# A hybrid decoder block on one core: where four of its modulation sums, the prefix sum of log f and some small transposes are computed

## The chip, the cores and the metric

The kernel runs on one core of a Trainium2 chip, as one launch. The metric is device time in microseconds; the time given for a kernel is the median of its runs. One more execution is recorded by the hardware profiler. Its span reaches from the first to the last instruction, and its own time is a little longer.

## What is computed

A decoder block for one sequence, all in float32, cut to what matters here. `mod` is the adaptive modulation: silu(c) times a 1024 x 6144 matrix, six vectors of 1024.

```python
mod = silu(c) @ w_ada + b_ada
sh1, sc1, g1, sh2, sc2, g2 = split(mod, 6)

h = rmsnorm(x, norm1_g) * (1 + sc1) + sh1
cb, cc, cv, q, k, v, f_logit, ga, gb = split(h @ w_in, IN_OFFSETS)
ya = cb * causal_dwconv(cc * cv, conv_a_w)
q, k = rmsnorm(q per head, q_norm_g), rmsnorm(k per head, k_norm_g)
log_f = log_sigmoid(f_logit + b_f)
F = cumsum(log_f, axis=sequence)           # 1024 positions x 8 heads
yb = softmax(q k^T / 8 + F[t] - F[s], causal) v
merged = sigmoid(ga) * (ya @ w_branch_a) + sigmoid(gb) * (yb @ w_branch_b)
x = x + g1 * (merged @ w_out)

h2 = rmsnorm(x, norm2_g) * (1 + sc2) + sh2
gate, val = split(causal_dwconv(h2 @ w_up, conv_ffn_w), 2)
x = x + g2 * ((silu(gate) * val) @ w_down)  # d_ff = 2816
```

## The kernel before

Sequence and model width are 1024, so x, h and most weights come as eight blocks (ND, NT) of 128. A product of float32 matrices is made of three matmuls on a high and a low part of each operand (TERMS: high x high, high x low, low x high). ACT copies the high part out (wsplit L93, h_tile L309), DVE or POOL subtract it to get the low part (L94, L312 on POOL, L315 on DVE).

Stages, in the span's time. **Head** (0 to 42 us): x is loaded, normed, transposed. **k loop** (to about 80): for dd = 1 to 7 one block of the contraction of k for seven tokens of 128 positions (k_mm, L326). Each step needs the modulation's shift and scale for block dd. These come from `ada_mul` (L220): two 512 KB blocks of w_ada, in [128 x 2 x 128] slices for eight k, are scaled by silu(c) and summed by DVE into two accumulators in SBUF, the even and the odd slices (two tensor_scalars L224, six scalar_tensor_tensors L226), and these are added (L229). `ada_sum` (L235) then sums over the partitions by two matmuls of one column against ones, into the bank `pm`. h_mod on ACT takes a and b from it, h_tile makes h's next block. With every odd dd, POOL splits the next unit of w_in (L94). In steps 3 to 5 a row of conv weights (`rw`) is transposed on PE, in step 6 the two norm gains (`rg`).

**V phase** (91 to 148): v for eight tokens, eight steps each (`tok_mm`, L530). **Q phase** (148 to 213): q for eight tokens. In both, small work is placed by hand: `at(t, f)` calls f before the matmuls of step t; steps count from TV = 8 for v and from TQ = 72 for q, eight to a token, about 0.7 us each in Q. So a token's sum of squares, root and norm (`sums`, `root`, `norm` on DVE), its transposition (`turn`, PE, qT), and its high and low parts (`high` on ACT, `low` on DVE, L493) stand at offsets from its first step. The remaining modulation blocks, the list `rest` (columns 16 to 47 in pairs), are loaded by `rest_load`, multiplied in four parts by DVE, ACT and POOL (`rest_mul`: L434, L437 on DVE, L438 ACT, L439 and L441 POOL), and summed over partitions by `late_pm`: five pairs in V, six in Q (NQ), five in the stage behind. `log_f`, `f_sum` and `f_turn` make the prefix sum F: f_sum multiplies log f by an upper triangle (`pf`) and by ones (`po`), and adds the totals of the blocks of 128 positions by eight small DVE operations; f_turn transposes it.

Behind that come the other products of w_in (to 350 us), attention (to 640), the mixing, the **up projection** (to about 1241; per f of 22 a tile of 128 gate and 128 value columns, by seven half-size products p1 to p7) and the **down projection** (77 steps of about 2.72 us). In a tile of the up projection the sums of DVE named c11, u2, u34, c12 and c21 put the products together, `scale`, `taps` and `silu` apply the convolution to the tile before, and `ff` multiplies its halves. POOL sums weights (L1593 to L1604), ACT and DVE split them (L1559, L1560).

Inside `manual_schedule` the order of the code is the order on each engine; SP, which issues most transfers, is ordered by hand in the head, k, V and Q phases, and by the scheduler in the up projection. The lines that steer the pieces named above:

```python
rest, rest_open, rest_sum, rest_acc = list(range(16, 48, 2)), [], [], []
at(t0 + 12, late_pm)      # V
at(TQ + 19, f_sum)
at(TQ + 21, f_turn)
at(t0 + 16, late_pm)      # Q
```

## Time and profile before

| what | value |
|---|---|
| time, median of 3 runs | 1474.64 us (1472.72 to 1478.87) |
| the profiled execution | 1473.5 us, span 1471.5 us |
| PE busy | 1403.4 us, 95% |
| DVE / ACT / POOL busy | 1099.4 / 651.8 / 504.1 us |
| mean granted clock of TensorE | 0.989 |
| DMA | 222.44 MB, mean 151 GB/s |

The page's first part gives an engine's busy time; what it does not tell is when the engine was idle, and that is read from the windows and timelines. In a timeline a row is one instruction or a run of equal ones, with start, duration, engine, line and names, and in square brackets the idle time ahead of it and what ended that. PE's fp32 matmul is run as two instructions, so a `pm` pair is shown as x4. The granted clock (PEclk) is a share of full speed.

### The profile page before, as it was taken

To read this page: it belongs to the slowest core of one execution; us is meant where nothing else is said; L and a number is where in the kernel's file an instruction comes from. 1 tells how busy PE (TensorE), PEld (TensorE's weight loads), DVE (VectorE), ACT (ScalarE), POOL (GpSimd) and SP (SyncE) were. 2 spreads that over 40 slices of the span, in tenths; PEclk is the share of its full clock that TensorE was granted. 3 is DMA by queue.
4 is the path that set the end of the run, shared out by engine and by line. 5 is a ranking of instruction groups with operands and counts; after the bars stand their busy time and mean duration, and the time that the engine had idled before them with its cause. 6 is when DMAs were issued, how large, how long until landed. Compare 5 with 4: busy or idle time off the path is not lost. (4 is left out here: it accounts for less than half of the span.)

```text
span 1471.5 us, 19375 instructions
## 1 busy us (share of the span) xinstructions
PE 1403.4 (95%) x6668; PEld 1155.1 (78%) x6668; DVE 1099.4 (75%) x1828; ACT 651.8 (44%) x1104; POOL 504.1 (34%) x532
## 2 busy tenths in 40 slices
PE   5889889999999999899999999999999999999997
PEld 4679668887888888778788877888888887888876
DVE  7965798888777776456846858777777776898764
ACT  6554453434455454555414534333333333444443
POOL 3646666665555553323221013333333331000000
PEclk9999999999999999999999999999999999999999
DMA  9539654437664557776962122222222213983722
GB/s 286 160 105 322 199 163 129 132 95 209 159 169 115 146 133 227 225 244 219 244 164 83 44 72 86 86 87 86 86 86 86 72 36 116 390 311 103 213 80 77
DMA packets 260759, 222.44 MB, mean 151 GB/s; under 512 B 43117, under 2 KB 213445, under 8 KB 260661
## 3 DMA queue, kind: packets, MB, share of 16 engines
q1 hardware_dynamic: 259389, 218.61, 49.6%
q0 software_dynamic: 1136, 2.56, 0.6%
q8 instruction: 52, 0.85, 0.2%
q14 instruction: 46, 0.38, 0.1%
q10 hardware_dynamic: 136, 0.04, 0.0%
HBM read 169.76 MB, written 51.41 MB: 150 GB/s over the span
## 5 line engine op out<-in xcount | busy, mean ns | idle before, releaser
L1925 PE MATMUL dn<-bL,aH 128*128 128x512 f32 x308 | 120.5, 391 | 0.6 <-DVE bL L1919 0.6
L1925 PE MATMUL dn<-bH,aH 128*128 128x512 f32 x308 | 120.8, 392 | 0.0
L1925 PE MATMUL dn<-bH,aL 128*128 128x512 f32 x308 | 120.0, 390 | 0.0
L1559 ACT ACTIVATE wh<-ws 128x512 fp32r<-128x512 f32 x95 | 55.5, 627 | 133.8 <-POOL ws L1593 131.0
L730 DVE TENSOR_TENSOR ol<-ws,oh 128x512 fp32r<-128x512 f32 x98 | 94.6, 974 | 14.1 <-ACT oh L729 11.6
L94 DVE TENSOR_TENSOR wl<-ws,wh 128x1024 fp32r<-128x1024 f32 (+1 forms) x51 | 70.0, 1373 | 40.6 <-ACT wh L93 40.1
L729 ACT ACTIVATE oh<-ws 128x512 fp32r<-128x512 f32 x98 | 61.2, 626 | 70.9 <-PE pacc L775 38.6
L1593 POOL TENSOR_TENSOR ws<-ws 128x512 f32<-128x512 f32 x19 | 24.7, 1300 | 187.7 <-DVE wl L94 187.7
L1162 ACT ACTIVATE L<-L,mn 128x256 f32<-128x256 f32 (+6 forms) x56 | 46.4, 829 | 60.7 <-DVE mn L1160 58.9
L1165 POOL TENSOR_SCALAR L<-L,rs 128x384 f32<-128x384 f32 (+7 forms) x62 | 48.3, 779 | 69.8 <-DVE rs L1164 68.6
L1925 PEld LDWEIGHTS dn<-bL,aH 128*128 128x128 f32 x308 | 57.8, 188 | 14.1 <-DVE bL L1919 2.7
L1185 ACT ACTIVATE th<-pt 128x512 fp32r<-128x512 f32 (+1 forms) x80 | 43.5, 551 | 55.3 <-PE pt L1179 53.7
L559 POOL TENSOR_TENSOR ws<-ws 128x512 f32<-128x512 f32 x42 | 55.1, 1312 | 36.5 <-DVE ol L730 17.1
L1925 PEld LDWEIGHTS dn<-bH,aH 128*128 128x128 f32 x308 | 57.8, 188 | 12.3 <-ACT bH L1918 0.4
L1925 PEld LDWEIGHTS dn<-bH,aL 128*128 128x128 f32 x308 | 57.8, 188 | 11.9
L93 ACT ACTIVATE wh<-ws 128x1024 fp32r<-128x1024 f32 (+1 forms) x58 | 60.8, 1052 | 12.3 <-DMA ws<-in_w_branch_a_dram 4.1
L1560 DVE TENSOR_TENSOR wl<-ws,wh 128x512 fp32r<-128x512 f32 x76 | 64.2, 864 | 2.3 <-ACT wh L1559 2.3
L1918 ACT ACTIVATE aH<-dws 128x512 fp32r<-128x512 f32 x52 | 32.8, 631 | 74.6 <-issue 41.0
L1680 DVE SCALAR_TENSOR_TENSOR u<-upv,cwT,u 128x1023 f32<-128x1023 f32 (+1 forms) x44 | 56.4, 1282 | 10.7 <-ACT u L1676 9.9
L1186 DVE TENSOR_TENSOR tl<-pt,th 128x512 fp32r<-128x512 f32 (+1 forms) x80 | 50.3, 634 | 18.5 <-ACT th L1185 17.1
L439 POOL TENSOR_TENSOR wacc<-wacc,wa 128x256 f32<-128x256 f32 x48 | 43.5, 907 | 55.8 <-ACT wa L438 52.4
L1919 DVE TENSOR_TENSOR aL<-dws,aH 128x512 fp32r<-128x512 f32 x52 | 35.9, 690 | 34.2 <-ACT aH L1918 34.2
(561 smaller groups left out, 4503.0 us busy)
## 6 DMA issues: line engine op xcount, KB each, us to landing
wa<-in_w_ada_dram SPq DMA_DIRECT2D x48, 512.0 KB
dws<-in_w_down_dram SPq DMA_DIRECT2D x96, 256.0 KB
ws<-in_w_up_dram SPq DMA_DIRECT2D x44, 512.0 KB
ws<-in_w_in_dram SPq DMA_DIRECT2D x36, 512.0 KB
ff<-ff_d SPq DMA_DIRECT2D x44, 256.0 KB
ff_d<-u SPq DMA_DIRECT2D x21, 512.0 KB
xt<-in_x_dram SPq DMA_DIRECT2D x8, 512.0 KB
v_d<-vt SPq DMA_DIRECT2D x8, 512.0 KB
```

Source lines behind the costliest of these rows:

```text
L93: scalar.activation(wh[:, : n * m], ws[:, : n * m], AF.Copy)
L94: eng.tensor_tensor(out=wl[:, : n * m], in0=ws[:, : n * m], in1=f32(wh[:, : n * m]), op=ALU.subtract)
L559: gpsimd.tensor_tensor(out=o, in0=a, in1=b, op=ALU.subtract)
L729: scalar.activation(h, src, AF.Copy)
L730: eng.tensor_tensor(out=l, in0=src, in1=f32(h), op=ALU.subtract)
L1162: scalar.activation(L[:, :n], L[:, :n], AF.Exp, scale=-1.0, bias=mn, accum_out=sm)
L1165: eng.tensor_scalar(out=L[:, :n], in0=L[:, :n], scalar1=rs, scalar2=0.0, op0=ALU.mult, op1=ALU.add)
L1186: vector.tensor_tensor(out=flat[2][:, c0:], in0=flat[0][:, c0:], in1=f32(flat[1][:, c0:]), op=ALU.subtract)
L1559: scalar.activation(ops[0][:, sl], src, AF.Copy)
L1560: eng.tensor_tensor(out=ops[1][:, sl], in0=src, in1=f32(ops[0][:, sl]), op=ALU.subtract)
L1680: vector.scalar_tensor_tensor(out=u[:, s:], in0=acc[:, : S - s], scalar=cwT[:, 2 - s, n : n + 1], in1=u[:, s:], op0=ALU.mult, op1=ALU.add)
L1925: mm(banks[e], self.A[i][:, es_], self.B[j], start=self.p in FIRST and self.c == 0 and t == 0, stop=self.c == NC - 1 and t == 2, skip_grou ...
```

## The change

- **k's sums.** `hT`, one bank of PSUM, holds pm in its first two columns and an accumulator of 256 columns behind them. `ada_chain` sums all eight slices into this one accumulator, each operation reading what the one before wrote; the eighth writes to SBUF. It is made in two parts around h_tile(dd + 1, 0), and behind h_mod(dd + 1), which reads the same bank.
- **Small transposes.** The rows of the gains and conv weights are loaded into the pool of the V phase, behind the fetches of v's first units. The gains are turned together at step 5, the three rows of conv weights at step 29 with one copy.
- **log f.** f_sum accumulates eight matmuls into pf: the triangle, then ones against ever shorter parts of log f. One DVE copy is left. f_turn comes 13 steps later.
- **Modulation pairs and q tokens.** `rest` ends at column 39, Q takes two pairs instead of six. late_pm comes 3 steps later in V and 6 in Q. The q tokens 0 to 5 go in pairs: one sum, root and norm for two, and two turns in two banks.
- **g2.** Its eight blocks of w_ada (512 KB each) are loaded in the up projection, one per tile from f = 5 on. In the next tile ACT scales the eight slices (four ahead of silu, four behind split4), POOL folds them by three adds to 128 columns, and at step 7 of the down projection (T0 + 1) eight matmuls of one column and one DVE add finish g2.

What stands on DVE in the k loop before (L224, L226, L229: ada_mul; L315: the low part of h):

```order
L224 TENSOR_SCALAR wacc<-wa,cT 128x256 x2
L226 SCALAR_TENSOR_TENSOR wacc<-wa,cT,wacc 128x256 x6
L229 TENSOR_TENSOR wacc<-wacc 128x256
L315 TENSOR_TENSOR h01L_118<-raw_187,h01H_114 128x512
L224 TENSOR_SCALAR wacc<-wa,cT 128x256 x2
```

And now (L238 and L243: the chain; hT is the bank):

```order
L238 TENSOR_SCALAR hT<-wa,cT 128x256
L243 SCALAR_TENSOR_TENSOR hT<-wa,cT,hT 128x256 x6
L243 SCALAR_TENSOR_TENSOR wacc<-wa,cT,hT 128x256
L329 TENSOR_TENSOR h01L_118<-raw_187,h01H_114 128x512
L238 TENSOR_SCALAR hT<-wa,cT 128x256
```

The two forms take the same places; seven of the eight operations now write to PSUM. On PE in the Q phase before, around the first token's transposition (L235 pm, L483 qT, L632 and L634 f_sum):

```order
L530 MATMUL qacc<-wl,h11H_131 128x512
L530 MATMUL qacc<-wh,h11L_135 128x512
L235 MATMUL pm<-ones,wacc 128x1 x2
L483 MATMUL qT<-ident,qn 128x128 x4
L530 MATMUL qacc<-wh,h01H_112 128x512
...
L530 MATMUL qacc<-wh,h01L_118 128x512
L632 MATMUL pf<-lf,upper 128x64
L634 MATMUL po<-lf,ones 128x64
L530 MATMUL qacc<-wh,h01H_115 128x512
```

And now (L658, L660: f_sum; L249 pm; L509 qT; two q tokens per pair):

```order
L556 MATMUL qacc<-wh,h01L_118 128x512
L658 MATMUL pf<-lf,upper 128x64
L660 MATMUL pf<-lf,ones 128x56
...
L660 MATMUL pf<-lf,ones 128x8
L556 MATMUL qacc<-wh,h01H_115 128x512
...
L556 MATMUL qacc<-wh,h11L_133 128x512
L249 MATMUL pm<-ones,wacc 128x1 x2
L556 MATMUL qacc<-wh,h11H_130 128x512
...
L509 MATMUL qT<-ident,qn 128x128 x4
...
L509 MATMUL qT<-ident,qn 128x128 x4
```

pm and the first qT moved behind f_sum, by 26 and 35 rows of PE, and the second token's qT now stands seven rows behind the first. On POOL in a tile of the up projection there were five instructions (L1560 a low part, L1593 to L1604 the sums of weights):

```order
L1560 TENSOR_TENSOR wl<-ws,wh 128x512
L1593 TENSOR_TENSOR ws<-ws 128x512
L1594 TENSOR_TENSOR ws<-ws 128x512
L1599 TENSOR_TENSOR ws<-ws 128x512
L1604 TENSOR_TENSOR ws<-ws 128x512
```

And now eight (L1858: the adds of g2):

```order
L1595 TENSOR_TENSOR wl<-ws,wh 128x512
L1858 TENSOR_TENSOR wa<-wa 128x512
L1858 TENSOR_TENSOR wa<-wa 128x256
L1858 TENSOR_TENSOR g2s<-wa 128x128
L1628 TENSOR_TENSOR ws<-ws 128x512
L1629 TENSOR_TENSOR ws<-ws 128x512
L1634 TENSOR_TENSOR ws<-ws 128x512
L1639 TENSOR_TENSOR ws<-ws 128x512
```

The adds stand between the low part of one weight and the sums for the next tile. The diff:

```diff
@@ -186,9 +186,9 @@
-    def rows_in(srcs, nm, eng=gpsimd, m=P):
-
-        st = xp.tile([P, P], F32, name=nm)
+    def rows_in(srcs, nm, eng=gpsimd, m=P, pool=None):
+
+        st = (pool or xp).tile([P, P], F32, name=nm)
         o = 0
@@ -228,6 +228,20 @@
         return acc[0]
+
+    def ada_chain(wa, part):
+
+        sums = hT[:, 256:512].rearrange("p (i m) -> p i m", i=2)
+        for k in range(4 * part, 4 * part + 4):
+            src, c1 = wa[:, :, k, :], cT[:, k : k + 1]
+            if k == 0:
+                vector.tensor_scalar(out=sums, in0=src, scalar1=c1, scalar2=None, op0=ALU.mult)
+                continue
+            out = sums
+            if k == ND - 1:
+                out = ap.tile([P, 2, P], F32, tag="wacc0", name="wacc", bufs=1)
+            vector.scalar_tensor_tensor(out=out, in0=src, scalar=c1, in1=sums, op0=ALU.mult, op1=ALU.add)
+        return out
@@ -366,25 +380,19 @@
     h_ada(4)
+    hT = aux_tile("hT")
     k_mm(0, (4, 5, 6), TERMS[:1])
-    h_mod(1, ada_sum(wc[1], aux_tile("pm")))
+    h_mod(1, ada_sum(wc[1], hT))
+    ada_chain(was[2], 0)
     k_mm(0, (4, 5, 6), TERMS[1:])
-    qk_rows = []
-    for nm, dst, src, f in (("rk", kg, k_norm_g, 1.0), ("rq", qg, q_norm_g, -0.125)):
-        qk_rows.append((rows_in([src, src], nm, sync, HD), dst, f))
-    cw_rows = [rows_in([conv_ffn_w[0, t].rearrange("(n p) -> n p", p=P)], f"rw{t}", sync) for t in range(3)]
-    wc[2] = ada_mul(was[2])
+    h_tile(1, 0)
+    wc[2] = ada_chain(was[2], 1)
     h_ada(5)
-    h_tile(1, 0)
     h_tile(1, 1)
...
     for dd in range(1, ND):
-        if dd + 2 < ND:
-            wc[dd + 2] = ada_mul(was[dd + 2])
-        if dd + 5 < ND:
-            h_ada(dd + 5)
         if dd == 2:
@@ -397,23 +405,41 @@
             units[dd // 2 + 1] = wsplit(kraw[dd // 2 + 1], gpsimd)
-        h_mod(dd + 1, ada_sum(wc[dd + 1], aux_tile("pm")))
+        h_mod(dd + 1, ada_sum(wc[dd + 1], hT))
+        if dd + 2 < ND:
+            ada_chain(was[dd + 2], 0)
         h_tile(dd + 1, 0)
+        if dd + 2 < ND:
+            wc[dd + 2] = ada_chain(was[dd + 2], 1)
+        if dd + 5 < ND:
+            h_ada(dd + 5)
         h_tile(dd + 1, 1)
         k_mm(dd, range(7), TERMS[1:])
-        if 3 <= dd < 6:
-            scalar.activation(cwT[:, dd - 3, :], rows_T(cw_rows[dd - 3], "rw"), AF.Copy)
-        elif dd == 6:
-            for (st, _), dst, f in qk_rows:
-                pt = aux_tile("rg")
-                tensor.transpose(pt[:HD, 0:2], st[0:2, :HD], ident[0:2, 0:2])
-                for r in range(2):
-                    scalar.activation(dst[r * HD : r * HD + HD], pt[:HD, r : r + 1], AF.Copy, scale=f)
     headS.close()
...
     bp = bS.enter_context(tc.tile_pool(name="qkv", bufs=1, side="right", reuse_waits="tile"))
+
+    qk_rows = []
+    for nm, dst, src, f in (("rk", kg, k_norm_g, 1.0), ("rq", qg, q_norm_g, -0.125)):
+        qk_rows.append((rows_in([src, src], nm, sync, HD, bp), dst, f))
+    cw_rows = [rows_in([conv_ffn_w[0, t].rearrange("(n p) -> n p", p=P)], f"rw{t}", sync, pool=bp) for t in range(3)]
+
+    def gains():
+
+        pt = aux_tile("rg")
+        for i, ((st, _), dst, f) in enumerate(qk_rows):
+            tensor.transpose(pt[:HD, 2 * i : 2 * i + 2], st[0:2, :HD], ident[0:2, 0:2])
+        for i, ((st, _), dst, f) in enumerate(qk_rows):
+            for r in range(2):
+                scalar.activation(dst[r * HD : r * HD + HD], pt[:HD, 2 * i + r : 2 * i + r + 1], AF.Copy, scale=f)
+
+    def cw_turn():
+        pt = aux_tile("rw", "aux2")
+        for t, (st, n) in enumerate(cw_rows):
+            tensor.transpose(pt[:, P * t : P * t + n], st[:n, :], ident[:n, :n])
+        scalar.activation(cwT, pt[:, : 3 * P].rearrange("p (t n) -> p t n", t=3)[:, :, : 2 * NF], AF.Copy)
@@ -448,7 +474,7 @@
-    rest, rest_open, rest_sum, rest_acc = list(range(16, 48, 2)), [], [], []
+    rest, rest_open, rest_sum, rest_acc = list(range(16, 40, 2)), [], [], []
     late_pm = lambda: rest_end(aux_tile("pm", "aux2"))
@@ -586,7 +612,7 @@
     nz, u, w, lw, m, num, den, lf = (small(n) for n in "nz u w lw m num den lf".split())
-    tot, Fs = nz, w
+    Fs = w
     FT = bp.tile([64, P], F32, name="FT")
@@ -629,15 +655,10 @@
         pf = aux_tile("pf")
-        mm(pf[:, :64], upper, lf, start=True, stop=True)
-        po = aux_tile("po", "aux2")
-        mm(po[:, :64], ones, lf, start=True, stop=True)
-        vector.tensor_copy(tot, po[:, :64])
+        mm(pf[:, :64], upper, lf, start=True, stop=False)
+        for j in range(1, NT):
+            mm(pf[:, 8 * j : 64], ones, lf[:, : 64 - 8 * j], start=False, stop=j == NT - 1)
         vector.tensor_copy(Fs, pf[:, :64])
-        for j in range(1, NT):
-            vector.tensor_tensor(out=tot[:, 8 * j : 8 * j + 8], in0=tot[:, 8 * j : 8 * j + 8],
-                                 in1=tot[:, 8 * j - 8 : 8 * j], op=ALU.add)
-        vector.tensor_tensor(out=Fs[:, 8:], in0=Fs[:, 8:], in1=tot[:, :56], op=ALU.add)
@@ -657,6 +678,8 @@
     at(0, kt[0].square, kt[1].square)
+    at(5, gains)
+    at(29, cw_turn)
     at(5, lambda: sums(kt[:2]))
@@ -688,7 +711,7 @@
                 at(t0 + 4 + i, lambda i=i: rest_mul(i))
-            at(t0 + 12, late_pm)
+            at(t0 + 15, late_pm)
         if j:
@@ -880,11 +903,11 @@
-    NQ = 6
+    NQ = 2
     NA, NB, NL = 10, 2, 1
...
     at(TQ + 19, f_sum)
-    at(TQ + 21, f_turn)
+    at(TQ + 34, f_turn)
     for i in range(9):
@@ -900,19 +923,29 @@
                 at(t0 + 6 + i, lambda i=i: rest_mul(i))
-            at(t0 + 16, late_pm)
+            at(t0 + 22, late_pm)
         acc = ps.tile([P, 512], F32, tag="qacc", name="qacc", bufs=6)
...
         qt.append(t)
-        if n < 7:
-            at(t0 + 10, t.square)
+        if n == 7:
+            break
+        at(t0 + 10, t.square)
+        if n == 6:
             at(t0 + 10, lambda t=t: sums([t]))
...
             at(t0 + 12, t.norm)
-            tt = t0 + (15 if n == 6 else 16)
-            at(tt, t.turn)
-            at(tt + 0, t.high)
-            at(tt + 1, t.low)
+            at(t0 + 15, t.turn)
+            at(t0 + 15, t.high)
+            at(t0 + 16, t.low)
+        elif n % 2:
+            two = qt[n - 1 : n + 1]
+            at(t0 + 10, lambda two=two: sums(two))
+            at(t0 + 11, lambda two=two: root(two))
+            at(t0 + 12, two[0].norm, two[1].norm)
+            for i, t in enumerate(two):
+                at(t0 + 17 + 2 * i, lambda i=i, t=t: t.turn(aux_tile("qT", ("aux", "aux2")[i])))
+                at(t0 + 17 + 2 * i, t.high)
+                at(t0 + 18 + 2 * i, t.low)
     qt[7].keep = ap.tile([P, 4, 512], F32R, tag="wa", name="q7", bufs=2)
@@ -1384,6 +1417,8 @@
+    g2p = ctx.enter_context(tc.tile_pool(name="g2", bufs=1, side="right", reuse_waits="tile"))
+    g2s = g2p.tile([P, ND, P], F32, name="g2s")
     upS = ExitStack()
@@ -1806,8 +1841,26 @@
     u2.scale_g()
+    FG = 5
+
+    def g2_load(b):
+        t = up.tile([P, S], F32, tag="u", name="wa", bufs=8)
+        t = t.rearrange("p (k m) -> p k m", k=ND)
+        sync.dma_start(t, kview(w_ada[0], (40 + b) * P, P))
+        return t
+
+    def g2_mul(t, ks):
+        for k in ks:
+            scalar.activation(t[:, k], t[:, k], AF.Copy, scale=cT[:, k : k + 1])
+
+    def g2_add(t, b):
+        for n in (4, 2, 1):
+            gpsimd.tensor_tensor(out=t[:, :n] if n > 1 else g2s[:, b : b + 1], in0=t[:, :n], in1=t[:, n : 2 * n], op=ALU.add)
+
+    wa = None
     for f in range(N0, NF):
         u, bf = U[f], U[f - 1]
+        ga, g2b = wa, f - 1 - FG
         nx = U[f + 1] if f + 1 < NF else None
@@ -1817,6 +1870,8 @@
         bf.taps_g()
+        if ga is not None:
+            g2_mul(ga, range(4))
         u.p2()
@@ -1825,6 +1880,9 @@
         u.split4()
+        if ga is not None:
+            g2_mul(ga, range(4, ND))
+            g2_add(ga, g2b)
         u.p5()
@@ -1836,6 +1894,7 @@
                 U[f + 2].fetch(up)
+            wa = g2_load(f - FG) if FG <= f < FG + ND else None
             nx.sums13()
@@ -1991,11 +2050,16 @@
         if st.c == 0 and t:
-            if n == 1:
-                sets.append(banks_for())
             done, old = steps[t - 1].p, sets[(n + 1) % 2]
...
         banks = sets[n % 2]
+        if t == T0 + 1:
+
+            sets.append(banks_for())
+            pm = sets[1][0]
+            for b in range(ND):
+                mm(pm[:, b : b + 1], g2s[:, b], ones[:, 0:1], start=True, stop=True)
+            vector.tensor_tensor(out=g2, in0=pm[:, :ND], in1=bada[:, 40:48], op=ALU.add)
         if t == T0:
```

## Rows read from the trace of the kernel before

**Rows 1.** The page's first part: busy time, share of the span, instructions:

```profile
PE 1403.4 (95%) x6668; PEld 1155.1 (78%) x6668; DVE 1099.4 (75%) x1828; ACT 651.8 (44%) x1104; POOL 504.1 (34%) x532
```

**Rows 2.** Windows, core 0: us, busy time by engine (instructions), PEclk, DMA share, GB/s:

```profile
80.40:91.00 10.60, 10.60 (x47) 8.60 (x48) 3.12 (x4) 6.08 (x11) 2.55 (x4) 1.00 0.04 5
91.00:147.70 56.70, 52.81 (x438) 52.02 (x437) 38.09 (x86) 27.38 (x59) 34.69 (x35) 1.00 0.93 279
...
162.00:172.00 10.00, 7.75 (x27) 6.22 (x27) 7.47 (x16) 4.38 (x10) 7.00 (x9) 0.66 0.47 126
...
1000.00:1025.00 25.00, 25.00 (x110) 20.37 (x109) 19.19 (x23) 7.76 (x11) 8.16 (x7) 1.00 0.40 125
```

**Rows 3.** PE's idle time: instruction, what it waited for, us, times, longest:

```profile
PE pm L235 <- DVE wacc L229: 7.8, 5, 4.2
...
PE qT L483 <- DVE qn L475: 5.8, 4, 1.9
...
PE pm L235 <- POOL wacc L441: 3.8, 2, 1.9
...
PE pF L644 <- DVE w L640: 2.0, 1, 2.0
...
PE qacc L530 <- DVE wl L94: 1.1, 1, 1.1
```

**Rows 4.** Timeline of PE, Q phase: start, us, instruction [idle before, releaser]:

```profile
164.79 1.09 PE L483 MATMUL qT<-ident,qn 128*128 128x128 f32 x4 [1.86 <-DVE qn L475]
165.53 0.78 PE L530 MATMUL qacc<-wh,h01H 128*128 128x512 f32 x1
...
169.52 0.52 PE L632 MATMUL pf<-lf,upper 128*128 128x64 f32 x2
...
211.99 0.63 PE L483 MATMUL qT<-ident,qn 128*128 128x128 f32 x4 [1.43 <-DVE qn L475]
```

**Rows 5.** Timeline of PE, k loop:

```profile
33.06 0.61 PE L235 MATMUL pm<-ones,wacc 128*128 128x1 f32 x4 [0.26 <-DVE wacc L229]
...
56.56 0.50 PE L235 MATMUL pm<-ones,wacc 128*128 128x1 f32 x4
...
60.36 0.25 PE L201 MATMUL rwp<-ident,rw 44*128 44x44 f32 x1
...
62.27 0.50 PE L235 MATMUL pm<-ones,wacc 128*128 128x1 f32 x4
...
75.80 0.58 PE L235 MATMUL pm<-ones,wacc 128*128 128x1 f32 x4 [1.92 <-DVE wacc L229]
```

**Rows 6.** Timelines of DVE and POOL, k loop:

```profile
38.57 2.87 DVE L315 TENSOR_TENSOR h01L<-raw,h01H 128x512 fp32r<-128x512 f32 x1
...
48.31 0.69 DVE L315 TENSOR_TENSOR h01L<-raw,h01H 128x512 fp32r<-128x512 f32 x1
...
38.34 5.40 POOL L94 TENSOR_TENSOR wl<-ws,wh 128x1024 fp32r<-128x1024 f32 x2
```

**Rows 7.** Line L437 (duration min/median/max) and a group of DVE by line and shape:

```profile
L437 DVE SCALAR_TENSOR_TENSOR wacc<-wa,cT,wacc x48: 469/485/908, 109.9 to 314.1; 128x256 f32<-128x256 f32 x48
...
L493 DVE SCALAR_TENSOR_TENSOR ql<-qT,kg,qh 128x512 fp32r<-128x512 f32 x8 | 6.0, 749 | 3.2 <-ACT qh L490 3.2
```

**Rows 8.** Groups of ACT and POOL by line and shape: us in all, mean ns:

```profile
L1162 ACT ACTIVATE L<-L,m 128x128 f32<-128x128 f32 x8 | 3.2, 400 | 9.4 <-DVE m L1152 9.4
...
L1593 POOL TENSOR_TENSOR ws<-ws 128x512 f32<-128x512 f32 x19 | 24.7, 1300 | 187.7 <-DVE wl L94 187.7
```

**Rows 9.** Timelines of DVE and PE, one tile of the up projection:

```profile
998.46 1.21 DVE L1705 TENSOR_TENSOR u<-u 128x1024 f32<-128x1024 f32 x1
...
1001.25 0.70 DVE L1625 TENSOR_TENSOR upg<-upg,s 128x512 f32<-128x512 f32 x1 [1.58 <-PE upg L1569]
1001.99 0.69 DVE L1625 TENSOR_TENSOR U<-upg,s 128x512 f32<-128x512 f32 x1
...
1003.80 0.39 PE L1569 MATMUL upg<-B22H,wh 128*128 128x512 f32 x1
```

## The prediction

> **What bounds the kernel now.** I read the engines' shares first. PE is busy 1403.4 of 1471.5 us [rows 1], so a change can gain only where PE sits idle or runs at its low clock, or by giving PE less to do. The windows show what "full" looks like: in the up projection at 1000 to 1025 us PE is busy for all 25.00 us and starts 110 matmuls, 0.227 us each, and the same window leaves DVE, ACT and POOL 5.8, 17.2 and 16.8 us free [rows 2]. Then I read what PE waited for. Of its 68 us of idle time the edited code owns 7.8 (pm on DVE's sums), 5.8 (qT on the norms), 3.8 (pm on POOL's sums) and 2.0 (pF) [rows 3]; the reader should see that these are few and long, and find each of them again in the timelines. [...]
>
> **Part 1: k's sums in PSUM, k loop (33 to 80 us).** PE's timeline has one pm per iteration, at 33.06, ..., 56.56, 62.27, ..., 75.80. From 33.06 to 75.80 is 42.74 us for six iterations; an undisturbed one is 62.27 - 56.56 = 5.71, of which one transpose (0.25 busy) is moved away, so 5.5 are left [rows 5]. The rest is two gaps, 4.2 and 1.92 [rows 3, 5], and slow matmuls after the first. Both gaps have one reason: DVE and POOL hold each other up when both work on SBUF. While POOL's two splits of weights run (5.40 us from 38.34), DVE's L315 takes 2.87 us instead of 0.69 [rows 6]. The new chain has one SBUF operand, the other in PSUM. DVE's L493, which reads PSUM, never shows such a stretch: its eight instructions average 749 ns, while the pure SBUF form L437 runs from 469 to 908 [rows 7]. So I let the chain be undisturbed and cost it at one tensor_scalar (0.5) and seven dependent operations of 0.52 (0.485 and a small gap): 4.1 us. L315 still has two SBUF inputs and is still hit.
>
> [...]
>
> L493 (512 elements, PSUM) and L437 (256, SBUF) differ by 264 ns for 256 elements, so both have a fixed part near 0.22 us, and I add nothing for PSUM; the other end is rival 1. The order of DVE stays chain, split, chain, split, but a chain can now start only after ACT has read pm out of the shared bank, and what queues behind that wait on DVE is L315. In an even iteration chain and split are 4.1 + 0.7 = 4.8 us, inside PE's 5.5. In an odd one POOL's split of weights (2.6 us) starts at the moment L315 does: 4.1 + 2.9 = 7.0, so PE waits 1.5. Six iterations are 3 x 5.5 + 3 x 7.0 = 37.5 instead of 42.74: **-5.2**. The last iteration also loses the gains' two transposes and a wait of 0.4 for ACT between them; with the first at 0.2 each and the other small edges I take 0.9: **-6.1** at the start of the V phase. Below: if L315 is no longer hit, 3 x 1.5 = 4.5 more.
>
> **Part 2: transposes in the V phase (91 to 148 us).** The five small transposes are paid here, about 0.8 us with their copies, and their five DMAs now stand behind the fetches of v's weights on SP's queue. Removed is pm's wait of 1.81 at the late pm (half of the 3.8 [rows 3]). Neither decides: DMA is busy 0.93 of this stage at 279 GB/s, and just before, at 80.4 to 91, it is busy 0.04 [rows 2]. Its burst therefore begins with the end of the k loop and moves with it, but the burst is not shorter. The third unit of q's weights already makes PE wait 1.1 (qacc on wl [rows 3]); what V gains, that wait gives back. V and the first 12 us of Q: **0**, shifted as a whole. If the burst did not move, the 6.1 would go too (rival 3).
>
> **Part 3: Q phase (148 to 213 us).** Before, PE meets a pm on POOL's sums after 1.9 us of idling and, behind it, qT at 164.79 after 1.86 [rows 3, 4]. The order now has pm nine matmuls of 512 columns behind the new f_sum, and the first qT 34 rows later, some 7 us of cover. Gone: 1.9 + 1.86, and the nine matmuls at half speed, 3.99 - 2.04 = 1.95; sum **-5.7**. pF's 2.0: f_turn stands 13 steps (9 us) later and the nine small DVE operations are gone: **-2.0**. Of qT's 5.8, two waits in the middle of the phase (5.8 - 1.86 - 1.43 = 2.5) lie between paired tokens with five to seven steps (3 to 5 us) of cover now: **-2.5**. Four of six pm pairs leave Q; a pair is 0.50 busy at 56.56 [rows 5], and as a matmul's end runs some 0.14 into the next one's start (0.39 busy and 0.227 apart [rows 2, 9]) it holds PE for 0.36: **-1.4**. f_sum has eight matmuls for two; a small fp32 matmul is half of such a pair, 0.18, so 6 x 0.18 = **+1.1**. The wait of 1.43 before the last qT [rows 4] grows, because on DVE two low parts (0.75 each, [rows 7]) now stand ahead of its norm: **+0.8** (0 to 1.5). The first paired qT may come up short: **+0.6** (0 to 1.2). The wait of the last token, q7, has the same neighbours and stays. Q: **-9.1**.
>
> **Part 4: g2 beside the up projection (from f = 5 on, eight tiles of 19.4 us).** Per tile: eight ACT scalings of 128x128, 400 ns by the nearest row, and three POOL adds of 512, 256 and 128 columns, 1.30 for the first and at most as much again for the two small ones [rows 8]: 3.2 and 2.6 us, far below the idle time, but they stand in order. Four scalings stand ahead of silu and the weight splits, so DVE's low parts come up to 1.6 us later, and ff (two SBUF inputs, 1.21) can be held 1.3 by POOL's first add. DVE has 1.58 us idle behind ff, and u2 ends at 1002.68, 1.1 before the product p3 takes the bank that u2 reads, at 1003.80 [rows 9]. Delay 1.6 + 1.3 = 2.9 against 1.58 + 1.1 = 2.7: the cover just about holds, 0 to 0.2 per tile, and if the second product slips as well 0.3. I take **+1.0** for all (0 to 2.5). The 512 KB load per tile meets a DMA share of 0.40 [rows 2]; SP issues it behind the fetch of the next tile, ten us before ACT needs it.
>
> **Part 5: the end of g2 in the down projection.** Eight fp32 matmuls at 0.18 on a full PE: **+1.45** (these replace the four pm pairs saved above). The one DVE add is 0.15 and waits for them with the next split behind it; the splits run two steps (5.4 us) ahead.
>
> **Clock.** New or remaining gaps of 1.5 to 2 us (three in the k loop, the qT of the end) may each be followed by slow matmuls, as after 164.79; I add **+1.0** (0 to 4).
>
> **Sum.** -6.1 + 0 - 9.1 + 1.0 + 1.45 + 1.0 = -11.75. From the profiled execution's 1473.5 that is 1461.75; the median shown, 1474.64, lies 1.1 above it and would give 1462.9. Predicted: **1462**.
>
> **Rivals.** (1) *The chain in PSUM is slow*: a read of what the operation before has just written costs more there than in SBUF. At 0.2 us per operation a chain is 5.7; odd iterations become 8.6 and even ones 6.4: 3 x 1.6 + 3 x 0.9 = 7.5 back, **1469**. Against: L493's duration; for: no row shows an accumulation in PSUM by DVE. (2) *Q's waits come back at the pairs*: two qT short by 1.5 with slow matmuls after the first (2): 5 back, **1467**. For: the root of two tokens waits for the later one. (3) *V's transfers do not move*: the k loop's 6.1 returns as PE waiting on wl: **1468**. Against: the 0.04 before. (4) *Slower, in the up projection*: silu, low parts and POOL's adds run one after the other ahead of u2, and the cover is used by something else. It decides from (11.75 + 7.4) / 8 = 2.4 us per tile; with all of 3.2 + 2.6 on the path less 1.1 it is 4.7 x 8 = 38 us: **1482 to 1500**. Against: DVE's u2 and p3 read nothing of g2. [...]
>
> **How the numbers follow.** Forecast 0.62 (1456 to 1467 by the bounds above); rival 1 0.07, rival 2 0.08, rival 3 0.07, rival 4 0.05, rival 5 0.11. A measurement of this kernel can tell about 0.5%, 7.4 us, from no change: faster is under 1467.3. Faster: 0.61 + 0.11 + 0.04 + 0.05 + 0.03 = 0.84; same 0.11; slower 0.05. The range 1454 to 1469 leaves out rival 4 and the ends of the others.
>
> **What would show it.** Right: pm in the k loop with waits of about 1.5 in odd iterations alone and none of 4; k's last iteration starting near 74.3; no pm, pF or qT wait between 150 and 185 and the granted clock near 1.00 there; PE still busy 25.00 of 25 between 960 and 1125. Wrong: chain operations above 0.6 us each (rival 1), a qacc wait on wl near 7 (rival 3), upv or upg waiting on U or wl in f = 6 to 13 (rival 4), or an L329 of 0.69 in odd iterations (rival 5).

## The result and the profile after

The changed kernel takes 1459.59 us (median, 1458.79 to 1463.72) against 1475.16 us (1472.72 to 1478.87): a ratio of 0.9898, 95% interval 0.987 to 0.9926, so 15.6 us less; the sum forecast 11.75. The profiled execution has a span of 1458.3 us. Its page answers to [rows 1]:

```profile
PE 1399.7 (96%) x6680; PEld 1154.3 (79%) x6680; DVE 1086.3 (74%) x1779; ACT 661.9 (45%) x1147; POOL 515.2 (35%) x540
```

PE has 3.7 us less to do, and 9.5 us less idle time. What PE waited for (us, times, longest), beside [rows 3]:

```profile
PE qT L509 <- DVE qn L501: 7.2, 2, 5.7
...
PE hT L249 <- DVE wacc L243: 4.1, 4, 1.1
...
PE pacc L509 <- DVE q L501: 2.1, 1, 2.1
...
PE qacc L556 <- DVE wl L94: 1.5, 1, 1.5
```

The long waits of pm and the one of pF are gone, four short ones of about 1 us are left at pm (now in hT), and a new one is longer than any that was removed: 5.7 us before a qT. Where the 13.2 us of span came from is read from the first matmul of each stage in both traces:

| first matmul of | before | after | lead |
|---|---|---|---|
| k's last step | 80.42 | 73.06 | 7.4 |
| q (qacc) | 147.69 | 139.82 | 7.9 |
| the products behind q (pacc) | 213.16 | 201.46 | 11.7 |
| attention (sp) | 351.3 | 338.2 | 13.1 |
| the branches (br) | 658.4 | 641.4 | 17.0 |
| the mixing (mix) | 703.6 | 686.7 | 16.9 |
| the up projection (upv) | 803.1 | 789.0 | 14.1 |
| the down projection (dn) | 1241.8 | 1227.6 | 14.2 |
| the end | 1471.5 | 1458.3 | 13.2 |

So the k loop gave 7.4, V 0.5, Q 3.8, the products behind it 1.4; g2 cost nothing in the up projection and 1.0 in the down projection. The lead also grows by 3.9 in attention and shrinks by 2.8 in the mixing, where no line was changed. The granted clock differs there: 0.89 from 587 to 602 and 0.81 from 687 to 703, where the kernel before had 0.77 (600 to 615) and 1.00 (704 to 720). The way from the first sp to the first upv is 451.8 us before, 450.8 after, and between 448.6 and 454.2 in the experiments below, whatever was edited ahead of it. Its changes are told of as nobody's gain or loss.

**The k loop.** PE's pm of the seven iterations (the first four shown), beside [rows 5]:

```profile
33.03 0.61 PE L249 MATMUL hT<-ones,wacc 128*128 128x1 f32 x4 [0.17 <-DVE wacc L229]
...
38.49 0.61 PE L249 MATMUL hT<-ones,wacc 128*128 128x1 f32 x4 [0.89 <-DVE wacc L243]
...
45.09 0.60 PE L249 MATMUL hT<-ones,wacc 128*128 128x1 f32 x4 [1.04 <-DVE wacc L243]
...
50.54 0.60 PE L249 MATMUL hT<-ones,wacc 128*128 128x1 f32 x4
```

The iterations take 6.60 and 5.45 in turn; the first to the last pm is 36.2 us instead of 42.74. What DVE does in two of them:

```profile
34.22 0.49 DVE L238 TENSOR_SCALAR hT<-wa,cT 128x256 f32<-128x256 f32 x1 [0.63 <-ACT a L316]
34.74 3.11 DVE L243 SCALAR_TENSOR_TENSOR hT<-wa,cT,hT 128x256 f32<-128x256 f32 x6
...
38.35 2.55 DVE L329 TENSOR_TENSOR h01L<-raw,h01H 128x512 fp32r<-128x512 f32 x1
...
41.33 3.11 DVE L243 SCALAR_TENSOR_TENSOR hT<-wa,cT,hT 128x256 f32<-128x256 f32 x6
...
45.22 0.69 DVE L329 TENSOR_TENSOR h01L<-raw,h01H 128x512 fp32r<-128x512 f32 x1 [0.20 <-POOL raw L328]
```

From the start of its first operation to the end of its eighth the chain takes 4.2 us both times, although POOL splits weights from 37.98 to 43.19, beside the second of them; its 36 scalar_tensor_tensors that write to PSUM (all six chains) run from 487 to 490 ns. L329, which has two SBUF operands, takes 2.55 in the first iteration and 0.69 in the second; the next chain starts behind it, and so PE waits 1.04 before pm at 45.09. POOL's own work beside the chain is shorter than before: its low parts of h (L326) take 1.28 to 1.31 us each in the loop, where L312 took 1.28 to 1.94 beside the sums in SBUF, and its scalings (L328) 0.76 to 0.77, where L314 took 0.77 to 1.05.

**The Q phase.** DVE and PE at the first q token, beside [rows 4] (L460: the second modulation pair's first operation; L496: the two tokens' sums):

```profile
159.37 0.52 DVE L460 TENSOR_SCALAR wacc<-wa,cT 128x256 f32<-128x256 f32 x1 [5.41 <-PE pm L249]
...
161.37 1.27 DVE L496 TENSOR_REDUCE ss<-sq 128x8 f32<-128x512 f32 x2
```

```profile
158.77 0.50 PE L249 MATMUL pm<-ones,wacc 128*128 128x1 f32 x4
...
167.17 1.09 PE L509 MATMUL qT<-ident,qn 128*128 128x128 f32 x4 [5.70 <-DVE qn L501]
...
168.49 0.63 PE L556 MATMUL qacc<-wl,h01H 128*128 128x512 f32 x1
168.91 0.63 PE L556 MATMUL qacc<-wh,h01L 128*128 128x512 f32 x1
```

DVE stood still for 5.41 us in front of the second pair's tensor_scalar, until PE had run pm at 158.77: both pairs are summed into the same buffers wacc, and the change moved pm back by six steps, but not the second pair. Behind it in DVE's queue stood the tokens' sums; the first of their norms ended near 167, and PE waited. Behind that gap the matmuls are 0.42 us apart (168.49, 168.91, ...), and the window has a granted clock of 0.88 for it:

```profile
157.00:185.00 28.00, 22.30 (x102) 18.15 (x101) 14.85 (x31) 7.29 (x13) 8.43 (x8) 0.88 0.25 68
```

**The up projection.** One tile with g2's work, on DVE, POOL, ACT and PE, beside [rows 9]:

```profile
985.52 2.31 DVE L1740 TENSOR_TENSOR u<-u 128x1024 f32<-128x1024 f32 x1
...
988.48 0.69 DVE L1660 TENSOR_TENSOR U<-upg,s 128x512 f32<-128x512 f32 x1
```

```profile
985.36 3.07 POOL L1858 TENSOR_TENSOR wa<-wa 128x512 f32<-128x512 f32 x2 [0.92 <-ACT wa L1854]
```

```profile
980.33 1.27 ACT L1854 ACTIVATE wa<-wa,cT 128x128 f32<-128x128 f32 x4
```

```profile
989.69 0.39 PE L1604 MATMUL upg<-B22H,wh 128*128 128x512 f32 x1
```

ff is held for 1.1 us (2.31 instead of 1.21), DVE's idle 1.58 behind it is used up, and u2 ends 0.5 us before p3 starts. PE loses nothing: 25.00 of 25 in the window.

```profile
985.00:1010.00 25.00, 25.00 (x110) 20.36 (x109) 22.41 (x23) 10.90 (x20) 13.67 (x12) 1.00 0.45 126
```

### The profile page after: what moved, and what is told of

The parts are those of the page before. It is cut to its first block, busy times and chain, and to the rows that moved or that the text cites. A ratio compares the mean times of both kernels' runs of the same rounds, so it can differ in the third digit from the quotient of the medians.

```text
span 1458.3 us, 19429 instructions
## 1 busy us (share of the span) xinstructions
PE 1399.7 (96%) x6680; PEld 1154.3 (79%) x6680; DVE 1086.3 (74%) x1779; ACT 661.9 (45%) x1147; POOL 515.2 (35%) x540
## 5 line engine op out<-in xcount | busy, mean ns | idle before, releaser
L753 DVE TENSOR_TENSOR ol<-ws,oh 128x512 fp32r<-128x512 f32 x98 | 92.5, 952 | 15.0 <-ACT oh L752 11.7
L94 DVE TENSOR_TENSOR wl<-ws,wh 128x1024 fp32r<-128x1024 f32 (+1 forms) x51 | 70.2, 1377 | 36.8 <-ACT wh L93 36.7
L1595 DVE TENSOR_TENSOR wl<-ws,wh 128x512 fp32r<-128x512 f32 x76 | 69.6, 935 | 8.9 <-ACT wh L1594 8.9
L1984 PEld LDWEIGHTS dn<-bL,aH 128*128 128x128 f32 x308 | 57.9, 188 | 13.2 <-DVE bL L1978 1.5
L1595 POOL TENSOR_TENSOR wl<-ws,wh 128x512 fp32r<-128x512 f32 x19 | 24.6, 1297 | 109.3 <-ACT wh L1594 109.3
```

The lines of the kernel that those rows point to most:

```text
L94: eng.tensor_tensor(out=wl[:, : n * m], in0=ws[:, : n * m], in1=f32(wh[:, : n * m]), op=ALU.subtract)
L753: eng.tensor_tensor(out=l, in0=src, in1=f32(h), op=ALU.subtract)
L1595: eng.tensor_tensor(out=ops[1][:, sl], in0=src, in1=f32(ops[0][:, sl]), op=ALU.subtract)
L1984: mm(banks[e], self.A[i][:, es_], self.B[j], start=self.p in FIRST and self.c == 0 and t == 0, stop=self.c == NC - 1 and t == 2, skip_grou ...
```

## The experiments

Each was timed against the kernel before on the same chip. That kernel's median was 1474.3 to 1475.2 in all sessions, so medians of different experiments are compared directly; their 95% intervals say what such a difference is worth.

**One: the second modulation pair of Q behind the first tokens' sums.**

```diff
-                at(t0 + 6 + i, lambda i=i: rest_mul(i))
-            at(t0 + 22, late_pm)
+                at(t0 + (6, 16)[n] + i, lambda i=i: rest_mul(i))
+            at(t0 + (22, 25)[n], late_pm)
```

> The changed kernel with one edit: the second modulation pair of the Q phase is multiplied ten steps later (behind the sums, root and norm of the first two q tokens) and its late_pm three steps later. Theory A: the wait of 5.70 us before the first qT comes from DVE, which stands 5.41 us at 159.37 in front of the second pair's tensor_scalar until PE has read the first pair's sum out of the one buffer both use, with the tokens' sums queued behind it. Then DVE's idle time there is gone, qT(0) waits under 2.2 us, the slow matmuls behind it become fewer, and the time falls by 4 to 7 us to 1452.5 to 1455.5. Rival B: the pairing itself is late (the root of two tokens waits for the second one, and DVE's small operations are stretched by POOL). Then qT(0) still waits 4 us or more and the time stays above 1457.5.

1453.05 us, ratio 0.9851 (0.9817 to 0.9884), 6.5 less than the change; no run of it (1449.77 to 1455.77) is as slow as the fastest of the change (1458.79). DVE's sums and PE's first qT:

```profile
155.37 1.27 DVE L496 TENSOR_REDUCE ss<-sq 128x8 f32<-128x512 f32 x2
```

```profile
162.78 0.60 PE L509 MATMUL qT<-ident,qn 128*128 128x128 f32 x4
```

No idle time stands before qT, and the products behind q start at 195.1 instead of 201.5. From the first qacc to the first pacc the Q phase takes 54.1 us instead of 61.6. Theory A holds, B falls: the pairing itself is not late.

**Two: the same order, another buffer.** The second pair is summed in its own weight tile, so nothing waits for pm.

```diff
+        if part == 0 and b == 28:
+            rest_acc[0] = wa[:, :, 0, :]
```

> The changed kernel in its own order, but the second modulation pair of the Q phase is summed in place in its own weight tile instead of in the buffer that the first pair's sum still fills. Theory A (the one shared buffer makes DVE stand 5.4 us, and the q tokens' sums queue behind it): DVE no longer waits for PE there. What stays ahead of the sums is the second pair itself, whose weights land near 155.2, so its four operations end near 158 instead of 161.3, and the first qT waits about 2.5 us (1.5 to 3.5) instead of 5.70; 1455 to 1457.5. Rival B (another reason): qT(0) waits 5 us or more, 1459 or more.

```profile
155.42 1.34 DVE L462 TENSOR_SCALAR wa<-wa,cT 128x256 f32<-128x256 f32 x1 [0.95 <-DMA wa<-in_w_ada_dram]
...
159.86 1.27 DVE L498 TENSOR_REDUCE ss<-sq 128x8 f32<-128x512 f32 x2
```

```profile
164.85 1.09 PE L511 MATMUL qT<-ident,qn 128*128 128x128 f32 x4 [2.85 <-DVE qn L503]
```

```profile
157.00:185.00 28.00, 25.14 (x112) 20.43 (x112) 15.94 (x31) 8.40 (x15) 10.25 (x10) 0.88 0.30 81
```

The wait fell to 2.85, as expected; DVE's 5.41 are gone, 0.95 for a transfer is left. So the shared buffer explains half of the wait, and the pair's place in DVE's queue the other half. The time forecast for it, 1455 to 1457.5, was missed: it is 1460.2 us (0.9895, 0.9875 to 0.9914), the same as the change's. The trace shows two reasons. The matmuls behind the shorter gap are slow (0.42 us apart) up to about 171, as behind the longer one, ten of 512 columns instead of six, so the Q phase gains 1.6 us (60.0 instead of 61.6) and not 2.85. And behind the wait of 2.1 for q7, which no edit touched, the next 24 matmuls of 512 columns take 7.3 us (208.1 to 215.4), where the changed kernel took 5.9 (209.55 to 215.47, granted clock 1.00 from 208 to 220); the products lose 1.4 us there. The second has nothing to do with the gap.

**Three: the k loop's part alone**, on the kernel before (the chain in PSUM, and the small transposes in V, which the bank needs).

```diff
-            wc[dd + 2] = ada_mul(was[dd + 2])
...
+        if dd + 2 < ND:
+            ada_chain(was[dd + 2], 0)
         h_tile(dd + 1, 0)
+        if dd + 2 < ND:
+            wc[dd + 2] = ada_chain(was[dd + 2], 1)
...
+    at(5, gains)
+    at(29, cw_turn)
```

> The kernel before with only the k loop's sums in PSUM and the small transposes moved to the V phase; Q phase, log f's sum and g2 as before. Theory A (the gain of the k loop is carried through V unharmed): k's last step starts near 73.1 instead of 80.42, the first qacc near 140 instead of 147.69, total 1467 to 1468.5 against 1475.2. Rival B (the transfers of V do not move, the gain comes back as waits on q's weights): first qacc above 144, total 1471 or more.

1463.83 us (1462.39 to 1467.89), ratio 0.9934 (0.9915 to 0.9952), 10.5 us less in the medians; its profiled execution has a span of 1466.1, 5.4 less. The first qacc is at 140.2 and pacc at 205.9, a lead of 7.5 and 7.3. The gain went through V unharmed, and rival 3 falls. The median lies 3 us under theory A's total of 1467 to 1468.5; the profiled execution is the slowest of the six. Q's waits are the old ones:

```profile
154.80 0.60 PE L249 MATMUL pm<-ones,wacc 128*128 128x1 f32 x4 [1.93 <-POOL wacc L467]
157.72 1.09 PE L509 MATMUL qT<-ident,qn 128*128 128x128 f32 x4 [2.31 <-DVE qn L501]
```

**Four: the chain's accumulator in SBUF**, order as changed; the chain then shares no bank with pm.

```diff
-        sums = hT[:, 256:512].rearrange("p (i m) -> p i m", i=2)
+        if part == 0:
+            chain[:] = [ap.tile([P, 2, P], F32, tag="wacc1", name="wacc", bufs=1)]
+        sums = chain[0]
```

> The changed kernel with the chain's accumulator in one buffer of SBUF instead of PSUM, same order and same dependence of each operation on the one before. Theory A (PSUM helps because it takes the second SBUF operand away): operations that meet POOL's split of weights or its h low parts are stretched to 0.9 to 1.5 us, or POOL's are; waits of pm in odd iterations rise from 1.05 to 2 us or more, the k loop becomes 3 to 6 us longer, total 1462 to 1466. Rival B (the gain comes from the order, one chain without a closing add, and the moved transposes): waits as in the changed kernel, total 1459 to 1461.

```profile
34.42 6.88 DVE L247 SCALAR_TENSOR_TENSOR wacc<-wa,cT,wacc 128x256 f32<-128x256 f32 x7
...
44.38 5.00 DVE L247 SCALAR_TENSOR_TENSOR wacc<-wa,cT,wacc 128x256 f32<-128x256 f32 x7
...
50.28 7.10 DVE L247 SCALAR_TENSOR_TENSOR wacc<-wa,cT,wacc 128x256 f32<-128x256 f32 x7
```

```profile
41.36 1.01 PE L253 MATMUL hT<-ones,wacc 128*128 128x1 f32 x4 [3.68 <-DVE wacc L247]
```

The seven operations take 6.88 and 7.10 us where POOL splits weights and 5.00 where it makes only h's low part, against 3.7 in PSUM. PE waits up to 3.68 before pm, the first qacc is at 149.0, later than before the change (147.7), and the time is 1471.08 us (0.9981, 0.9965 to 0.9997). Theory A holds, with more than its price (1462 to 1466): up to the first qacc the order alone gains nothing, and PSUM is worth 9.1 us (149.0 against 139.8).

**Five: single q tokens**, on experiment one, each with its own sums, root, norm and turn at the old offsets.

```diff
-        elif n % 2:
-            two = qt[n - 1 : n + 1]
-            at(t0 + 10, lambda two=two: sums(two))
...
+        at(t0 + 10, lambda t=t: sums([t]))
+        at(t0 + 11, lambda t=t: root([t]))
+        at(t0 + 12, t.norm)
+        tt = t0 + (15 if n == 6 else 16)
+        at(tt, t.turn)
```

> e1 (second pair later) with the q tokens 0 to 5 taken one by one again, each with its own sums, root, norm and turn at the offsets of the kernel before. Theory A (pairs pay, because one root for two tokens saves five small DVE operations and the turn has five to seven steps behind the norm): two or more qT waits of 1.2 to 1.9 come back, 2.5 to 5 us in all with slow matmuls behind the long ones, 1455.5 to 1459. Rival B (with only two modulation pairs left in Q, DVE is free enough for single tokens): qT waits as in e1, 1451.5 to 1454.5.

```profile
158.89 1.12 PE L509 MATMUL qT<-ident,qn 128*128 128x128 f32 x4 [6.32 <-DVE qn L501]
```

1464.64 us (0.9925, 0.9903 to 0.9946), 11.6 more than with pairs, of which the first qT's 6.32 us are the largest part; three more waits of 0.3 to 1.2 follow. Theory A, but above its price (1455.5 to 1459). The largest part is not what the theory named: the pair's first turn stands nine steps later on PE, and a single token's doesn't, while its sums on DVE start only at 154.5, behind log f and the first modulation pair.

**Six: more POOL work in the up projection**, on experiment one: three adds of 512 columns, which g2 doesn't need, ahead of its own in eight tiles.

```diff
+        for _ in range(3):
+            gpsimd.tensor_tensor(out=t[:, :4], in0=t[:, :4], in1=t[:, 4:], op=ALU.add)
```

> e1 with three more POOL adds of 512 columns ahead of g2's in each of the eight tiles of the up projection (about 4.5 us more POOL work per tile; g2 comes out wrong). Theory A (my step: the cover of ff, c11 and u2 just about holds; u2 ends 0.52 us before p3 takes its bank in the changed kernel, so any more POOL time in front of it stands on PE's path): 4.0 us per tile, 32 in all, 1485. Rival B (only the stretch in which DVE's ff is held counts, POOL's later sums have six us of their own): 0 to 1 us per tile, 1453 to 1461, PE busy 25.00 of 25.

```profile
1009.43 4.96 POOL L1858 TENSOR_TENSOR wa<-wa 128x512 f32<-128x512 f32 x3 [0.92 <-ACT wa L1854]
1014.47 2.95 POOL L1860 TENSOR_TENSOR wa<-wa 128x512 f32<-128x512 f32 x2
```

```profile
1013.37 0.47 PE L1604 MATMUL upg<-B22H,wh 128*128 128x512 f32 x1 [0.61 <-DVE U L1660]
...
1017.33 0.50 PE L1604 MATMUL upv<-T4H,wh 128*128 128x512 f32 x1 [0.92 <-DVE upv L1660]
```

The adds take 4.96 us, PE waits 0.61 and 0.92 in the tile, and the up projection grows from 438.7 to 454.6 us, 2.0 per tile (0.5 of it is not shown as idle time); 1468.37 us (0.9952, 0.9935 to 0.9969). Neither theory: of 5 us, 3 were covered. The 0.5 us between u2 and p3 were not the whole cover. POOL's adds run on beside c11 and u2, which read PSUM and take 0.69 as ever; what they hold is ff (2.31, as in the changed kernel) and now the low part behind u2 too (L94, 2.33 instead of 1.22).

**Seven and eight: the waits of the last tokens**, on experiment one. The first pair's turns come three steps later, the seventh token's one step, the last one's two half products; a split of k's second weight unit that is made again at dd = 1 is left out.

```diff
-    units[1] = wsplit(kraw[1], gpsimd)
...
-            at(t0 + 15, t.turn)
+            at(t0 + 16, t.turn)
...
+                tt = t0 + 2 * i + (20 if n == 1 else 17)
+                at(tt, lambda i=i, t=t: t.turn(aux_tile("qT", ("aux", "aux2")[i])))
...
-            extra = {3: [lambda: qt[7].turn(new_acc())], 4: [qt[7].high], 5: [qt[7].low],
...
+            extra = {5: [lambda: qt[7].turn(new_acc())], 6: [qt[7].high, qt[7].low]
...
```

> The changed kernel with e1's edit, the first two q turns three steps later, the turn of the seventh q token one step and that of the last one two steps later, and without the first of two equal splits of k's second weight unit (it is split before the loop and again at dd = 1). Theory A: all three waits of qT and q7 (5.70, 1.48, 2.07) go with most of the slow matmuls behind them (about 2 us behind each long one), and the k loop loses one collision with POOL (1.0 to 1.6): 1459.6 - 5.7 - 1.5 - 2.1 - 1.3 - 2 = about 1447, range 1444 to 1451. Rival B: what waits behind these is DVE itself, so the waits move to the next consumer (products on low parts): 1453 or more.

1453.29 us (0.9861, 0.9836 to 0.9886), as experiment one. The split left out brought nothing to be seen: L329 still meets the one that is left (2.53 us), and the first qacc is at 140.2. The wait moved from q7's turn to a low part, as rival B said:

```profile
203.24 0.80 PE L797 MATMUL pacc<-wh,ol 128*128 128x512 f32 x1 [3.29 <-DVE ol L752]
```

So in the eighth run q7's sums, root and norm stand behind the splits for the next products:

```diff
-    qt[7].square()
-    sums(qt[7:])
-    root(qt[7:])
-    qt[7].norm()
     t23(T3, 0, 1)
...
+            extra = {0: [qt[7].square, lambda: sums(qt[7:])], 1: [lambda: root(qt[7:])], 2: [qt[7].norm],
+                     5: [lambda: qt[7].turn(new_acc())],
...
```

> e4 with the sums, root and norm of the last q token behind the splits that the next products need. Theory A (e4 only moved the wait: DVE's order puts q7's seven operations, stretched to 6 us by POOL, ahead of the low parts ol that PE asks for at 203.24): the wait of 3.29 goes, with some slow matmuls behind it: 1447 to 1450. Rival B (DVE is the bound of this stretch whatever its order): another low part or q7's norm is late by 2 us or more, 1452 to 1455.

```profile
202.93 0.66 PE L508 MATMUL pacc<-ident,q 128*128 128x128 f32 x4 [1.40 <-DVE q L500]
```

1451.3 us (0.9842, 0.9824 to 0.9859), between the times of the two theories: the wait for the low part is gone, and 1.4 for q7's norm are left. The time lies 2 us under the seventh run's, but the intervals overlap.

**Nine: POOL's splits in halves**, on the eighth.

```diff
+        c = n * m // 2 if eng is gpsimd and m == 512 else n * m
+        for o in range(0, n * m, c):
+            eng.tensor_tensor(out=wl[:, o : o + c], in0=ws[:, o : o + c], in1=f32(wh[:, o : o + c]), op=ALU.subtract)
```

> f5 with POOL's splits of k's and q's weights made in two halves of 512 columns. Theory A (in odd iterations DVE's low part of h stands behind POOL's whole split of 1024 columns, 2.5 us, and that is what PE's remaining waits of 1.05 before pm come from): the low part meets at most one half, takes 1.3 to 1.5 us instead of 2.5, the three waits of about 1.0 go, 2 to 3.5 us less than f5: 1448 to 1449.5. Rival B (DVE's next start is then set by ACT's reading of pm, or POOL loses as much at the second half): waits within 0.3 us of f5's, 1450.5 to 1452.

```profile
38.55 1.44 DVE L331 TENSOR_TENSOR h01L<-raw,h01H 128x512 fp32r<-128x512 f32 x1
```

```profile
38.69 0.61 PE L251 MATMUL hT<-ones,wacc 128*128 128x1 f32 x4 [0.17 <-DVE wacc L245]
...
44.18 0.61 PE L251 MATMUL hT<-ones,wacc 128*128 128x1 f32 x4
```

The low part L331 takes 1.44 instead of 2.5, pm has no wait from 44.18 on, every iteration takes 5.5 us, and the first qacc is at 136.6 instead of 140.1. The waits went as theory A said; of the time, 1450.19 us (1447.32 to 1453.59; 0.9838, 0.9814 to 0.9862), only 1.1 less in the medians can be seen, inside the scatter. By its median it is the fastest version of this study.

**Ten: log f's totals on DVE again**, on experiment one, f_turn at its new place.

```diff
-            mm(pf[:, 8 * j : 64], ones, lf[:, : 64 - 8 * j], start=False, stop=j == NT - 1)
+        mm(po[:, :64], ones, lf, start=True, stop=True)
...
+        for j in range(1, NT):
+            vector.tensor_tensor(out=tot[:, 8 * j : 8 * j + 8], in0=tot[:, 8 * j : 8 * j + 8],
+                                 in1=tot[:, 8 * j - 8 : 8 * j], op=ALU.add)
+        vector.tensor_tensor(out=Fs[:, 8:], in0=Fs[:, 8:], in1=tot[:, :56], op=ALU.add)
```

> e1 with log f's block totals added on DVE again (two matmuls and nine more small DVE operations), but with f_turn where the change has it, 13 steps later. Theory A (what removed pF's wait of 2.0 is f_turn's place; the sums on TensorE only cost PE 1.68 for 0.3 to 0.4): PE saves 1.3 us, pF does not wait, and the nine operations (3 to 4 us on DVE) stand between the sums and the roots of the first two tokens, so the first qT waits 0 to 3 us: 1452 to 1455. Rival B (DVE is the bound there and every us of it counts): qT(0) waits 3 us or more with slow matmuls behind it, 1455.5 to 1459.

In the kernel before, and here:

```profile
170.77 2.97 DVE L638 TENSOR_TENSOR nz<-nz 128x8 f32<-128x8 f32 x7
```

```profile
156.20 5.08 DVE L664 TENSOR_TENSOR nz<-nz 128x8 f32<-128x8 f32 x7
```

```profile
163.05 0.66 PE L509 MATMUL qT<-ident,qn 128*128 128x128 f32 x4 [2.48 <-DVE qn L501]
...
170.68 0.27 PE L670 MATMUL pF<-ident,w 128*64 128x128 f32 x1
```

pF doesn't wait (170.68), so f_turn's place is enough for that. But seven adds of eight columns take 5.08 us (2.97 before the change, where one of them took 1.29 beside a subtraction on POOL and most of the others 0.17), and the first qT waits 2.48: 1455.99 us (0.988, 0.9862 to 0.9897), 2.9 more than experiment one, with intervals that overlap. The wait is within A's bounds and the time just inside B's. The sum on TensorE costs PE 1.7 us and takes this wait away, because DVE is what the first tokens wait for.

**Eleven: g2 alone** moved, all else as before.

```diff
-    rest, rest_open, rest_sum, rest_acc = list(range(16, 48, 2)), [], [], []
+    rest, rest_open, rest_sum, rest_acc = list(range(16, 40, 2)), [], [], []
...
-    NQ = 6
+    NQ = 2
...
+    def g2_load(b):
```

> The kernel before with only g2 moved to the up projection (six modulation pairs in the Q phase become two); k loop, transposes, log f and single q tokens as before. Theory A: by itself this takes four pm pairs (1.4) from PE in Q and adds eight matmuls (1.2) in the down projection; the waits at the first token (pm, qT, pF) stay, the two later qT waits of 1.25 go: 1471 to 1474.5. Rival B (DVE's load in Q sets all of Q's waits): 6 us or more, under 1468.5.

1473.48 us (0.9994, 0.9979 to 1.0009): nothing, as theory A said, and the waits at the first token stay. In the profiled execution, the slowest of ten, pF even waits longer, because the seven adds ahead of it took 5.34 us here, where they took 2.97 in the kernel before:

```profile
172.17 5.34 DVE L638 TENSOR_TENSOR nz<-nz 128x8 f32<-128x8 f32 x7
```

```profile
166.19 1.08 PE L483 MATMUL qT<-ident,qn 128*128 128x128 f32 x4 [2.34 <-DVE qn L475]
...
177.70 0.42 PE L644 MATMUL pF<-ident,w 128*64 128x128 f32 x1 [4.28 <-DVE w L640]
```

## Why the prediction was right, point by point

The direction, the time (1462 for 1459.6) and the chain of reasons in the k loop held. That the total came so near is in part luck: the Q phase brought 5.3 us less than its term, and the k loop (1.3 more), V (0.5), the products (1.4), attention and mixing together (1.0), g2 (1.0 and 0.5) and the clock's 1.0 made up for it. Of the signs named for being right, one failed: between 150 and 185 us a qT waits, and the granted clock is not near 1.00.

- **k loop, -6.1; measured -7.4.** Right in mechanism and nearly in size. The chain is 4.2 us where 4.1 were worked out, and is not held by POOL. The odd iterations take 6.6 instead of 7.0, because L329 starts 0.37 us after the split and takes 2.55 instead of 2.9. The even ones are PE's 5.45. Six iterations gained 6.5 us, the last one 0.8. Experiment four shows that PSUM is the cause, experiment nine that L329 is the rest. Rival 1 (a slow chain) falls: 487 to 490 ns for each operation.

  For PSUM I had added nothing. In the traces the eighth operation, which reads PSUM and writes SBUF, takes 479 to 482 ns, and the six that also write PSUM 487 to 490, against a median of 479 in SBUF before (471 at the least, 1517 at the most). Beside POOL the difference is large: in experiment four, with the same operations, seven take 6.9 us in SBUF beside the splits, against 3.7 in PSUM. Rival 5 (L329 no longer hit, 4.5 us more gained) falls: L329 still takes 2.55 to 2.61 beside POOL's splits, 0.68 to 0.69 without them.

- **V, 0; measured -0.5.** Right. The transfers moved with the end of the k loop: from 91 to 100 the DMA share is 0.94, where it was 0.22 before, and a lead of 7.4 became 7.9; q's third unit makes PE wait 1.5 instead of 1.1.

- **Q, -9.1; measured -3.8.** The step that failed is the term "the first paired qT may come up short: +0.6 (0 to 1.2)". It is 5.70 and slow matmuls behind it. I had counted the cover of qT in steps of PE and left out that moving late_pm back by six steps also moves the release of the buffer that the second pair's first DVE operation needs, with the tokens' sums queued behind. For the k loop I had named what is queued behind an instruction that waits; here I did not. Rival 2 named the place (pairs short, slow matmuls behind), with another reason and at 1467. The other terms came as said: pm's and pF's waits and the two middle ones are gone, f_sum costs 1.70 for eight matmuls (0.21 each instead of 0.18), the last qT waits 1.48 instead of the 2.2 forecast. The 3.99 of the nine matmuls at half speed is PE's time from 165.53 to 169.52 before (0.43 us apart), the 2.04 nine times 0.227; now six slow ones, 0.42 apart, stand behind the 5.70.

- **The products behind Q, not forecast; -1.4.** q7's wait is the same 2.07, but the granted clock behind it is 1.00 (208 to 220), where 216 to 225 had 0.81. I had taken that stretch as unchanged. The gain is not the change's: with the same order and a wait of 2.1 experiment two has the slow matmuls again (7.3 us for 24, against 5.9).

- **Up projection, +1.0; measured 0.** The delay of ff and the small remaining slack of u2 came as worked out (2.31 us, 0.5 us); that it "just about holds" was too narrow by some 3 us (experiment six). Rival 4 falls.

- **Down projection, +1.45; measured 1.0.** The eight pairs of instructions are busy for 1.84 us in all, ends overlapping:

```profile
L2061 PE MATMUL dn<-ones,g2s 128*128 128x1 f32 x16 | 1.8, 245 | 0.0
```

- **Clock, +1.0.** Not separable: the k loop has no stretch with a granted clock under 1.00 any more (0.82, 0.83 and 0.76 from 33 to 59 before, 1.00 now), Q has one (0.88 from 157 to 185), attention and mixing change by 2 to 4 us between kernels that differ in nothing there. That slow matmuls follow a gap is shown of some gaps only: they are 0.43 us apart behind the 1.86 at 164.79 before (granted clock 0.51 from 164.6 to 170.5) and 0.42 behind the 5.70 now (0.50 from 166.9 to 171), but 0.23 behind the 1.43 at 211.99 before and the 1.48 at 200.29 now.

## What to carry to other kernels

A DVE chain that runs beside GpSimd work is worth trying with one operand in PSUM: here the same seven operations took 3.7 us there and 6.9 in SBUF. When a consumer is moved later (here a matmul that frees a buffer), look at who fills that buffer next and what is queued behind it, since that engine now waits for the moved one. And a gap on TensorE that is halved may win less than was cut from it (1.6 us in the Q phase for 2.85), because the matmuls behind it are slow too (0.42 us apart here, in either case); without the gap the phase was 7.5 us shorter.
